# A matmul with a decayed running sum: from the fifth pair of chunks on, x is turned by transposing DMAs, and the output leaves in lumps of eight slots

## The chip, the cores and the metric

The kernel runs on one core of a Trainium2 chip. The metric is the time of one execution on the device in microseconds (us). The engines are named as in the profile: PE (TensorE, the matmuls), PEld (its weight loads), DVE (VectorE), ACT (ScalarE), POOL (GpSimd) and SP (SyncE, which here only issues DMAs). SP, ACT and POOL each have a queue of their own from which they start DMAs; an engine works through its instructions in order.

## What is computed

```python
B, S, D = (16, 2048, 1024)          # x: (16, 2048, 1024), w: (1024, 1024), decay: (1024,)
xw = x @ w
out[:, 0, :] = xw[:, 0, :]
for t in range(1, S):
    out[:, t, :] = decay[None, :] * out[:, t - 1, :] + xw[:, t, :]
```

All inputs and the output are float32. The kernel multiplies in bfloat16 and sums in float32.

## The kernel before

The work is cut into 64 chunks of 512 time steps (`TL`), four for each of the 16 batches. Two chunks make a group; there are 32 groups. For each group the kernel goes through eight column blocks `n` of 128 output columns each. One (group, block) pair is a slot; the last group is done chunk by chunk, so there are 31 x 8 + 2 x 8 = 264 slots. PE computes in one slot the product for 128 output columns (on the partitions) and 1,024 time steps: 8 pieces of the inner dimension times 2 chunks, 16 matmuls of 512 columns.

**How x gets in.** The matmul needs x with its inner dimension on the partitions. `load` (L105) brings one quarter of a chunk with one DMA from POOL, casting float32 to bfloat16: 32 partitions hold time steps, and a run is 256 columns of x, so four DMAs make a chunk in a tile `xb` (ring of 3). `turn` (L115) is a DVE transpose in blocks of 32 x 32 of pairs of bfloat16 into `xw` (ring of 2). `part` (L123) is an ACT copy in two halves that separates the pairs into `xt` (ring of 5), which the matmuls (L131) read. The partition order that comes of this is matched by the order in which w lies in `wsb`.

**What happens to a product.** Two kinds of slot alternate by a fixed rule. In an unpaired slot DVE runs the scan with the decay straight from PSUM (L221). In a paired slot, of which there are three in four, ACT copies the product to `xs` (L183) and makes decay times the even steps (L169); POOL adds them to the odd steps (`join`, L196); DVE scans only the odd steps with the square of the decay (L201); ACT multiplies again (L169), and POOL fills in the even steps (`fill`, L246). The last value of each row is kept for the next group of the same batch (L250). Then `back` (L258) turns the result on DVE in 32 x 32 blocks into an output tile `ot`.

**How the output gets out.** An `Outlet` collects four slots in one `ot` tile (ring of 4). When its fourth slot has been turned, `store` (L282) issues four DMAs of 512 KB from SP, one for each quarter of the partitions, with runs of 512 bytes in DRAM. Only at the end of the run some stores go out from POOL as well.

**What sets the order.** Every operation is pinned in program order on its engine. After each slot's matmuls, `perform` runs a list of deeds, each a letter with a number: P (copy, even part, join), S (scan), C (complete), B (back), T (turn a chunk), X and Y (its two part copies), L (one load). For slots 0 to 33 and for the last 20 the lists are written out by hand (`agenda`); between them `usual` makes them, and `later` says at which slot T, X and Y of a chunk come: 11, 10 and 8 slots ahead of the group's first slot for its first chunk, 7, 6 and 4 for its second. After T of chunk c the loads of chunk c+3 are put in line, and L takes them one or two a slot. At the end `ending` turns the last tiles on PE and stores them in four DMAs with rows of 2 KB (L393).

Of the kernel before, what the change touches and what calls it, by code (L numbers as in the profile page):

```python
# [22 lines left out]


@with_exitstack
def kernel(
# [7 lines left out]

# [38 lines left out]
    dec = const.tile([128, K], FP32, name="dec")  # L89
    squares = [const.tile([128, K], FP32, name="squares")]  # L90
    wsb = const.tile([128, K, K, NQ, P], BF16, name="wsb")
    wcols = wsb.rearrange("p k (h r) q i -> p k h q r i", h=2)

    def ot_tile(nj):
        return ring(sb, "ot", 4, [128, nj, CR])
# [4 lines left out]

    def load(c, q, j0=0, j1=NJ):
        b, t0 = chunks[c]
        if c not in xb_of:
            xb_of[c] = ring(sb, "xb", 3, [128, NJ, CQ], BF16)
        pin(nc.gpsimd.dma_start(  # L105
            out=xb_of[c][quad(q), j0:j1],
            in_=_ap(x, [[D, P], [P * D, j1 - j0], [1, CQ]],
                    (b * S + t0 + j0 * P) * D + q * CQ)))

# [9 lines left out]
    def part(c, copy, m0, m1, j0=0, j1=NJ):  # L119
        if c not in xt_of:  # L120
            xt_of[c] = ring(sb, "xt", 5, [128, M, 2, TL], BF16)
        src = xw_of[c][:, m0:m1, j0:j1].rearrange("p m j i e -> p m e (j i)")
        pin(copy(out=xt_of[c][:, m0:m1, :, j0 * P:j1 * P], in_=src))  # L123

    def matmul(ps, n, k, xt, t0=0, t1=TL, start=0, pairs=None):
# [4 lines left out]
        lhs = wsb[:, k, n].rearrange("p q i -> p (q i)")  # L130
# [10 lines left out]
    class Tile:  # L141

        def __init__(self, g, n, ps, outlets):
            self.b, self.t0 = chunks[g[0]]
            self.T = TL * len(g)
            self.n, self.ps, self.outlets = n, ps, outlets
            self.paired = n % R != R - 1
# [17 lines left out]
        def decayed(self, src):  # L167
# [3 lines left out]
                scale=dec[:, self.n:self.n + 1]))  # L171
# [26 lines left out]
        def scan(self):  # L198
            T, n, so = self.T, self.n, self.so
            if self.paired:  # L200
                pin(nc.vector.tensor_tensor_scan(  # L201
                    out=so[:, 3:T + 2:2],
                    data0=squares[-1][:, n:n + 1].to_broadcast([128, T // 2]),
# [11 lines left out]
        def run(self, ps, t, size):  # L215
            n, so = self.n, self.so
            if t:
                before = so[:, t + 1:t + 2]
            else:
# [3 lines left out]
                data0=dec[:, n:n + 1].to_broadcast([128, size]),  # L223
# [28 lines left out]
        def back(self, half=None):  # L252
            n, c0 = self.n, self.n % R * P
            for outlet in self.outlets:
                if half not in (None, outlet.half):
                    continue
                t0, nj = outlet.t0, outlet.nj
                pin(nc.vector.transpose(  # L258
# [7 lines left out]
    class Outlet:  # L266


        def __init__(self, ns, nj, half=0, queues=(nc.sync,), pieces=1):
            self.pieces = pieces  # L270
            self.ns, self.missing, self.half = ns, set(ns), half
            self.nj, self.t0, self.queues = nj, half * nj * P, queues
            self.ot = ot_tile(nj)

        def store(self, b, t0):
            n0 = self.ns[0]
            c0 = n0 % R * P
            size = len(self.ns) * P
            nj = self.nj // self.pieces
            for j in range(0, self.nj, nj):  # L280
                for i, q in enumerate((0, 2, 1, 3)):
                    pin(self.queues[i % len(self.queues)].dma_start(  # L282
                        out=_ap(out, [[D, P], [P * D, nj], [1, size]],
                                (b * S + t0 + self.t0 + j * P) * D
                                + n0 // R * CH + q * CR + c0),
                        in_=self.ot[quad(q), j:j + nj, c0:c0 + size]))


# [63 lines left out]
    def decays(i):  # L352
        pin(nc.vector.transpose(out=cols, in_=rows))
        pin(nc.vector.tensor_copy(
            out=dec.rearrange("p (h r) -> p h r", h=2), in_=cols[:, :, 0:R]))
        square(0)

    def square(i):
        pin(nc.vector.tensor_tensor(
            out=squares[-1][:, 0:K], in0=dec, in1=dec, op=ALU.mult))  # L360
# [4 lines left out]


# [8 lines left out]
    def ending(i):  # L375
# [7 lines left out]
        def cross(blocks, rs):  # L383
# [6 lines left out]
        def leave(i, copy):  # L390
# [3 lines left out]
                out=_ap(out, [[D, 128], [1, CH]], (b * S + t0 + i * 128) * D + CH),  # L394
                in_=wides[i].rearrange("p q r i -> p (q r i)")))

        cross((0,), range(R))
        cross((1,), range(R))
        cross((2, 3), range(R - 1))
        cross((2, 3), (R - 1,))  # L400
# [7 lines left out]
    def turn_and_load(c):  # L408
        turn(c)
        if 2 <= c < nch - 3:  # L410
            loads.extend((c + 3, q) for q in range(NQ))
# [9 lines left out]
        "Y": lambda c: part(c, nc.scalar.copy, 2, M),  # L421
        "x": lambda c: part(c, nc.vector.tensor_copy, 0, 2),
# [35 lines left out]
        9: "k6 h6 c5 B4",  # L458
# [9 lines left out]
        19: "S16 j17 p18 B15 L g18 L S17 k16 h16 z18 j18",  # L468
        20: "Y7 S19 L c16 k17 h17 T8 k19 L c17",
        21: "p20 g20 L S18 X8 j20 B17 B19",  # L470
        22: "L h18 p21 c18 B16 k18 g21 B18 Y8 z20 L j21 S20",
        23: "p22 z21 z22 S21 L h20 g22 T9 c20 h21",
        24: "k21 k20 j22 S23 X9 L c21 Y9 B20 L",
        25: "B23 k23 p24 B21 g24 z24 j24 S22 z25",
        26: "p25 T10 k22 h22 g25 c22 S24 X10 j25",
        27: "B22 p26 S25 g26 z26 Y10 j26",
        28: "S27 h25 h24 c25 S26 c24",
        29: "B27 h26 c26 T11 p28 g28 j28 B24",
        30: "p29 B25 g29 z28 j29 S28 z29 S29",
        31: "h28 p30 c28 B26 g30 h29 B28 j30 z30",  # L480
        32: "c29 S31 S30 h30 B29 c30 p32 g32 z32 j32 B30 B31 L L",
        33: "p33 g33 z33 j33 S32 h32 c32 k32 L L",
# [23 lines left out]
    begun = {"T": 12, "X": 11, "Y": 11}  # L506
    for c in range(5, nch):
        first = c // 2 * K
        ahead = (7, 6, 4) if c % 2 else (11, 10, 8)
        for letter, a in zip("TXY", ahead):  # L510
            if c >= begun[letter]:
                later.setdefault(first - a, []).append(f"{letter}{c}")

    def usual(s):
# [11 lines left out]
        return do + later.get(s, []) + ["L"] * (2 if len(loads) > NQ else 1)  # L526

    def rest(s):
# [4 lines left out]
        return do + [f"B{s - 1}"] + later.get(s, []) + ["L"] * len(loads)  # L533
# [7 lines left out]
    for step, (g, n) in enumerate(slots):  # L541
        T = TL * len(g)
        left = step - len(slots)
        if n % R == 0:
# [95 lines left out]
```

## Time and profile before

| | |
|---|---|
| two timed runs | 908.58 and 909.44 us, median 909.01 |
| profiled execution, first to last instruction (its span) | 907.2 us |
| profiled execution, what lies around the span | not listed; the median of the runs is 1.8 us above the span |
| granted TensorE clock, mean | 0.998 |
| busy: PE / DVE / ACT / POOL | 892.8 / 826.3 / 686.2 / 663.0 us |
| matmuls L131 of 512 columns from `xt` | 859.8 us, 3,914 records |
| ACT copies L123 of 2,048 elements | 124, 1,904 ns each |
| DVE turns L115 of a whole chunk | 62, 2,285 ns each |
| DVE turns L258 of 1,024 steps | 248, 1,216 ns each |
| POOL issuing a load L105 | 264, 661 ns each |
| POOL issuing an output L282 | 8, 722 ns each |
| loads, 256 KB written each, issue to landing | 248, 7.8 us in the median |
| outputs, 512 KB each, issue to landing | 244 from SP, 10.9 us in the median |

All times come from one profiled execution on one core. "Busy" is the time in which an engine had an instruction running; a DMA that an engine issues is not counted in it. The page cuts the span into 40 slices of 22.7 us and gives the busy share of each in tenths. Landing is the time from a DMA's issue until its data have arrived. In the lists of waits the name left of the arrow is the engine that waited and the name right of it is what came last.

### The profile page before, as it was taken

What the parts mean: (1) busy time and instruction counts of PE and PEld (TensorE: products, weight loads), DVE (VectorE), ACT (ScalarE), POOL (GpSimd) and SP (SyncE); (2) the same over time, 40 slices, a digit from 0 to 9 for tenths busy, and PEclk for the clock granted to TensorE, in tenths of its full rate; (3) what the DMA queues carried; (4) which work ended last, traced back from release to release, by engine and by line L of the source; (5) the groups of instructions that cost most, each with busy time, mean ns of one, the idle gap of its engine ahead of it and who ended that gap; (6) DMA issues with size and microseconds to landing.
All of it is one profiled execution on the core that took longest, in us unless ns stands there. A gap on an engine that the chain in (4) does not pass through costs nothing.

```text
span 907.2 us, 12004 instructions
## 1 busy us (share of the span) xinstructions
PE 892.8 (98%) x4119; PEld 411.4 (45%) x4201; DVE 826.3 (91%) x628; ACT 686.2 (76%) x955; POOL 663.0 (73%) x763
## 2 busy tenths in 40 slices
PE   9999999999999999999999999999999999999996
PEld 5444444444444444444444444444444444444443
DVE  4999989999999999899999999999999999999996
ACT  4889867777777877877877778778778778777742
POOL 7888678877777767768677777777677686776562
PEclk9999999999999999999999999999999999999999
DMA  9999999999999999999999999999999999999788
GB/s 194 194 215 220 227 215 220 215 238 255 249 250 254 241 243 259 247 244 228 227 233 227 227 232 227 226 232 233 220 230 231 228 231 223 232 229 207 153 161 211
DMA packets 397230, 204.77 MB, mean 226 GB/s; under 512 B 8816, under 2 KB 395376, under 8 KB 397168
## 3 DMA queue, kind: packets, MB, share of 16 engines
q1 hardware_dynamic: 258960, 131.62, 59.6%
q0 software_dynamic: 137920, 71.85, 58.1%
q8 instruction: 33, 0.54, 0.2%
q10 hardware_dynamic: 288, 0.52, 0.2%
q14 instruction: 29, 0.24, 0.1%
HBM read 138.42 MB, written 134.22 MB: 301 GB/s over the span
## 4 chain that ended last, share of the span: by engine, by line
PE 93%; DMA 2%; POOL 1%; issue 1%; DVE 1%; ACT 0%; POOLq 0%; DVEq 0%
PE ps L131 93%; DMA xb<-in_x_dram 2%; POOL ot L299 1%; POOL xb L105 1%; PE spare L131 1%; DVE xw L115 0%; ACT xt L123 0%; ACT xs L183 0%; DVE so L201 0%; PE spare L387 0%; DVE ot L258 0%; ACT h L169 0%; PE ps L387 0%; POOLq L635 0%; POOL xs L196 0%
## 5 line engine op out<-in xcount | busy, mean ns | idle before, releaser
L131 PE MATMUL ps<-xt,wsb 128*128 128x512 bf16 x3942 | 863.5, 378 | 4.7 <-ACT h L169 0.2
L131 PEld LDWEIGHTS <-wsb 128*128 128x128 bf16 x4152 | 405.9, 98 | 479.9 <-ACT wsb L306 0.8
L196 POOL TENSOR_TENSOR xs<-h,xs 128x512 f32<-128x512 f32 (+1 forms) x190 | 243.0, 1279 | 181.8 <-ACT h L169 79.4
L183 ACT COPY xs<-ps 128x1024 f32<-128x1024 f32 (+1 forms) x190 | 189.4, 997 | 155.3 <-PE ps L131 144.2
L258 DVE STREAM_TRANSPOSE ot<-so 128x1024 f32<-128x1024 f32 (+1 forms) x260 | 300.1, 1191 | 2.1 <-POOL so L190 1.1
L246 POOL TENSOR_TENSOR so<-h,xs 128x512 f32<-128x512 f32 (+1 forms) x190 | 241.4, 1272 | 39.0 <-ACT h L169 25.7
L123 ACT COPY xt<-xw 128x2048 bf16<-128x2048 bf16 (+1 forms) x136 | 242.3, 1790 | 7.8 <-DVE xw L115 7.6
L105 POOL DMA_DIRECT2D xb<-in_x_dram x264 | 174.3, 661 | 3.3 <-DMA ot<-in_w_dram 1.1
L169 ACT ACTIVATE h<-so,dec 128x512 f32<-128x512 f32 (+1 forms) x190 | 145.4, 766 | 27.7 <-DVE so L201 24.4
L115 DVE STREAM_TRANSPOSE xw<-xb 128x2048 f32<-128x2048 f32 (+1 forms) x78 | 147.4, 1901 | 5.5 <-DMA xb<-in_x_dram 5.5
L201 DVE TENSOR_TENSOR_SCAN so<-spare,keep,xs 128x512 f32<-128x512 f32 (+1 forms) x97 | 120.0, 1239 | 27.7 <-POOL xs L196 27.4
L201 DVE TENSOR_TENSOR_SCAN so<-spare,xs 128x512 f32<-128x512 f32 x93 | 113.3, 1220 | 27.6 <-POOL xs L196 24.6
L169 ACT ACTIVATE h<-ps,dec 128x512 f32<-128x512 f32 (+1 forms) x190 | 130.3, 686 | 0.0
L221 DVE TENSOR_TENSOR_SCAN so<-dec,ps 128x1024 f32<-128x1024 f32 x34 | 76.8, 2261 | 1.0 <-ACT h L169 1.0
L221 DVE TENSOR_TENSOR_SCAN so<-dec,keep,ps 128x1024 f32<-128x1024 f32 (+1 forms) x35 | 75.9, 2169 | 0.1
L250 ACT COPY keep<-so 128x1 f32<-128x1 f32 x136 | 25.3, 189 | 9.9 <-DVE so L221 9.4
L192 ACT COPY so<-keep 128x1 f32<-128x1 f32 x97 | 18.4, 191 | 2.6 <-DVE ot L258 2.4
L131 PE MATMUL ps<-xw,wsb 128*128 128x256 bf16 (+1 forms) x68 | 11.2, 301 | 0.1
L190 POOL MEMSET so<- 128x1 f32 x93 | 10.7, 117 | 0.6 <-DVE ot L258 0.6
L131 PE MATMUL spare<-xt,wsb 128*128 128x512 bf16 (+1 forms) x48 | 10.0, 335 | 0.0
L282 POOL DMA_DIRECT2D out_dram<-ot x8 | 5.7, 722 | 5.5 <-DVE ot L258 5.1
L299 POOL DMA_DIRECT2D ot<-in_w_dram x12 | 6.6, 546 | 3.3 <-DMA xb<-in_x_dram 2.0
(38 smaller groups left out, 44.5 us busy)
## 6 DMA issues: line engine op xcount, KB each, us to landing
out_dram<-ot SPq DMA_DIRECT2D x244, 512.0 KB, 10.9
xb<-in_x_dram POOLq DMA_DIRECT2D x248, 256.0 KB, 7.8
xb<-in_x_dram POOLq DMA_DIRECT2D x16, 128.0 KB, 5.8
out_dram<-ot POOLq DMA_DIRECT2D x4, 512.0 KB, 11.6
ot<-in_w_dram POOLq DMA_DIRECT2D x12, 128.0 KB, 5.1
out_dram<-ot SPq DMA_DIRECT2D x4, 256.0 KB
out_dram<-ot POOLq DMA_DIRECT2D x4, 256.0 KB, 8.5
out_dram<-ot SPq DMA_DIRECT2D x8, 128.0 KB, 4.3
```

The source lines that it names most:

```text
L105: pin(nc.gpsimd.dma_start(out=xb_of[c][quad(q), j0:j1], in_=_ap(x, [[D, P], [P * D, j1 - j0], [1, CQ]], (b * S + t0 + j0 * P) * D + q * CQ)))
L115: pin(nc.vector.transpose(out=dst.rearrange("p (m j i) -> p j m i", m=M, i=P)[:, j0:j1, m0:m1], in_=src.rearrange("p (j m c) -> p j m c", ...
L123: pin(copy(out=xt_of[c][:, m0:m1, :, j0 * P:j1 * P], in_=src))
L131: pin(nc.tensor.matmul(out=ps[:, t0:t1] if ps.shape[1] >= t1 else ps, lhsT=lhs, rhs=rhs, start=(k == 0 and t0 == start), stop=(k == K - 1),))
L169: pin(nc.scalar.activation(out=h, in_=src, func=mybir.ActivationFunctionType.Copy, scale=dec[:, self.n:self.n + 1]))
L183: pin(nc.scalar.copy(out=self.xs, in_=self.ps))
L196: pin(nc.gpsimd.tensor_tensor(out=odds, in0=self.g, in1=odds, op=ALU.add))
L201: pin(nc.vector.tensor_tensor_scan(out=so[:, 3:T + 2:2], data0=squares[-1][:, n:n + 1].to_broadcast([128, T // 2]), data1=self.xs[:, 1:T:2 ...
L221: pin(nc.vector.tensor_tensor_scan(out=so[:, t + 2:t + 2 + size], data0=dec[:, n:n + 1].to_broadcast([128, size]), data1=ps, initial=befor ...
L246: pin(nc.gpsimd.tensor_tensor(out=self.so[:, 2:T + 2:2], in0=self.h, in1=self.xs[:, 0:T:2], op=ALU.add))
L250: pin(nc.scalar.copy(out=self.keep, in_=self.so[:, self.T + 1:self.T + 2]))
L258: pin(nc.vector.transpose(out=outlet.ot[:, :, c0:c0 + P], in_=self.so[:, 2 + t0:2 + t0 + nj * P].rearrange("p (i t) -> p i t", t=P)))
```

## The change

From chunk 8 (group 4, slot 32) on:

- A chunk of x is loaded by one DMA from POOL in whole rows of 4 KB, 128 time steps on the partitions, four such row blocks in the `xb` tile. SP then issues four transposing DMAs (`cross`), each of which takes one block of 128 rows x 1,024 bfloat16 from `xb` to `xt`, with 8 x 128 elements on each of 128 partitions. `turn` and `part` are no longer used for these chunks.
- The four transposes of a chunk come 7 slots (first chunk of a group) or 5 slots (second chunk) ahead of the group's first slot. The load of chunk c+3 is placed three slots behind the transposes of chunk c, whose `xb` buffer it takes.
- The inner dimension now lies in plain order and so do the output columns, so a second copy of the weights, `wsn`, is made in slots 19 to 31: two loads (N) and eight ACT copies (n). The decay and its square get a second copy as well (A).
- For groups 4 to 29 an outlet is a lump of eight slots: 1,024 columns and 1,024 time steps, 4 MB, in 1-KB runs. The `ot` ring is two lumps. When the lump is full, SP issues the quarters 0 and 2 at once; the quarters 1 and 3 are put in line, and POOL issues one of them in each of the next slots (O).
- `xt` has a ring of 4 in place of 5.
- The last tiles, turned on PE, go to DRAM in four runs of 512 bytes a row in place of one of 2 KB.

```diff
+    FIRST = 8
+    WIDE = range(FIRST // 2, nch // 2 - 2)
+
+    def crossed(c):
+        return c >= FIRST
+
+    def column(c, n):
+        return n * P if crossed(c) else n // R * CH + n % R * P
+
+    SPAN = {False: CR, True: CQ}
...
+    wsn = const.tile([128, K, K, NQ, P], BF16, name="wsn")
...
-    def ot_tile(nj):
-        return ring(sb, "ot", 4, [128, nj, CR])
+    def lump():
+        return ring(sb, "ot", 2, [128, 2, 2 * NJ * CR])
...
     def load(c, q, j0=0, j1=NJ):
         b, t0 = chunks[c]
         if c not in xb_of:
             xb_of[c] = ring(sb, "xb", 3, [128, NJ, CQ], BF16)
+        if crossed(c):
+            pin(nc.gpsimd.dma_start(
+                out=xb_of[c].rearrange("p (l j) c -> p l (j c)", l=NB),
+                in_=_ap(x, [[D, 128], [128 * D, NB], [1, D]], (b * S + t0) * D)))
+            return
...
+    def cross(c):
+        xt_of[c] = ring(sb, "xt", 4, [128, M, 2, TL], BF16)
+        rows = xb_of[c].rearrange("p (l j) c -> p l (j c)", l=NB)
+        cols = xt_of[c].rearrange("p m e t -> p (m e) t")
+        for l in range(NB):
+            pin(nc.sync.dma_start_transpose(
+                out=cols[:, :, l * 128:(l + 1) * 128], in_=rows[:, l]))
...
         def store(self, b, t0):
+            if len(self.ns) == K:
+                for q in (0, 2):
+                    self.send(nc.sync, q, b, t0)
+                for q in (1, 3):
+                    due.append(lambda q=q: self.send(nc.gpsimd, q, b, t0))
+                return
...
+        def send(self, queue, q, b, t0, j=0, nj=None):
+            nj = nj or self.nj
+            pin(queue.dma_start(
+                out=_ap(out, [[D, P], [P * D, nj], [1, len(self.ns) * P]],
+                        (b * S + t0 + self.t0 + j * P) * D
+                        + q * SPAN[crossed(self.c)] + column(self.c, self.ns[0])),
+                in_=self.ot[quad(q), j:j + nj]))
...
+    def fetch(i):
+        part = ring(sb, "xw", 2, [128, NB, D], BF16)
+        for l in range(NB):
+            wst[i * NB + l] = part[:, l]
+        pin(nc.gpsimd.dma_start(
+            out=part, in_=_ap(w, [[D, 128], [128 * D, NB], [1, D]], i * NB * 128 * D)))
+
+    def place(k):
+        pin(nc.scalar.copy(
+            out=wsn[:, k].rearrange("p n q i -> p q n i"),
+            in_=wst[k].rearrange("p (q n i) -> p q n i", q=NQ, n=K)))
...
             pin(nc.sync.dma_start(
-                out=_ap(out, [[D, 128], [1, CH]], (b * S + t0 + i * 128) * D + CH),
-                in_=wides[i].rearrange("p q r i -> p (q r i)")))
+                out=_ap(out, [[D, 128], [CQ, NQ], [1, CR]], (b * S + t0 + i * 128) * D + CR),
+                in_=wides[i].rearrange("p q r i -> p q (r i)")))
...
     def turn_and_load(c):
-        turn(c)
+        if crossed(c):
+            cross(c)
+        else:
+            turn(c)
         if 2 <= c < nch - 3:
-            loads.extend((c + 3, q) for q in range(NQ))
+            loads.extend((c + 3, q) for q in range(1 if crossed(c + 3) else NQ))
...
-    begun = {"T": 12, "X": 11, "Y": 11}
-    for c in range(5, nch):
-        first = c // 2 * K
-        ahead = (7, 6, 4) if c % 2 else (11, 10, 8)
-        for letter, a in zip("TXY", ahead):
-            if c >= begun[letter]:
-                later.setdefault(first - a, []).append(f"{letter}{c}")
+    for c in range(FIRST, nch):
+        at = c // 2 * K - (5 if c % 2 else 7)
+        later.setdefault(at, []).append(f"T{c}")
+        later.setdefault(at + 3, []).append("L")
...
-        return do + later.get(s, []) + ["L"] * (2 if len(loads) > NQ else 1)
+        return do + later.get(s, []) + ["O"] * (len(due) > 0)
...
-        if n % R == 0:
-            ns, nj = range(n, n + R), T // P
+        lot = K if g[0] // 2 in WIDE else R
+        if n % lot == 0:
+            ns, nj = range(n, n + lot), T // P
...
             for k, l in todo:
-                matmul(ps[:, l * TL:(l + 1) * TL], n, k, xt_of[g[l]])
+                matmul(ps[:, l * TL:(l + 1) * TL], n, k, xt_of[g[l]],
+                       of=wsn if crossed(g[l]) else wsb)
```

## The prediction

> **What bounds the kernel now.** I read the page's busy shares first, then the slices, the chain that ended last, the queue table, and last the waits of SP's own queue.
>
> ```profile
> PE 892.8 (98%) x4119; PEld 411.4 (45%) x4201; DVE 826.3 (91%) x628; ACT 686.2 (76%) x955; POOL 663.0 (73%) x763
> ...
> PE   9999999999999999999999999999999999999996
> ...
> DMA  9999999999999999999999999999999999999788
> GB/s 194 194 215 220 227 215 220 215 238 255 249 250 254 241 243 259 247 244 228 227 233 227 227 232 227 226 232 233 220 230 231 228 231 223 232 229 207 153 161 211
> ...
> q1 hardware_dynamic: 258960, 131.62, 59.6%
> q0 software_dynamic: 137920, 71.85, 58.1%
> ...
> PE 93%; DMA 2%; POOL 1%; issue 1%; DVE 1%; ACT 0%; POOLq 0%; DVEq 0%
> ```
>
> TensorE is busy in every slice but the last, and the chain is 93% TensorE. A busy PE need not be at its peak, so I checked the rate in the chain in order of time:
>
> ```profile
> 59.10 10.96 PE ps L131 x50
> 70.11 10.74 PE ps L131 x49
> ```
>
> The second piece is 49 matmuls in 10.74 us and the next starts 10.79 us after it: about 216 ns for each 512-column matmul, without a hole. A group of two chunks is 128 matmuls, 27.6 us, and a slot 3.45 us. So DVE, ACT and POOL work beside PE, and their work is worth nothing in time until it makes PE wait. The other thing to see is that the DMA engines too are busy in nine tenths of every slice; the shares of the two queues add up to 118%, so their packets overlap.
>
> The third view is what SP does, because the change puts new work there:
>
> ```profile
> SPq L282 <- DVE ot L258: 299.9, 50, 33.6
> ```
>
> ```profile
> L282 SPq DMA_DIRECT2D out_dram<-ot x256: 315/2622/6642, 38.7 to 900.2; - x128
> ...
> DMA to landing us min/median/max: 3.5/10.8/19.0
> ```
>
> The first line: SP spends 300 of 907 us waiting for DVE's output turns. The second (ns, min/median/max): one output DMA holds SP for 0.3 to 6.6 us, 2.6 in the median, and lands 10.8 us after issue. SP is a queue in order; whatever stands behind an output there waits with it.
>
> **The change, part by part** (durations from the groups by form, one group = 27.6 us).
>
> DVE loses 56 turns L115 of 2,285 ns (128 us); ACT loses 112 copies L123 of 1,904 ns (213 us) and gains 8 copies for the second set of weights, about 1 us each by half that row. POOL issues 1 load a chunk in place of 4 at 0.661 us: 56 x 3 x 0.66 = 111 us less, and 26 groups x 2 outputs x 0.72 us = 37 us more. All of this lies beside PE: worth 0. Matmul count and weight loads (98 ns each, under 216) stay: 0. The first 8 chunks keep their order: 0. Once only come four decay DMAs of 1 KB on SP (slot 9) and two loads of the second weights on POOL (slots 19 and 21, 0.66 us each; the second waits for the last turned chunk's copy in slot 20): hidden by the same POOL idle time, 0. At the very end four stores go from 2-KB rows to 512-byte runs, 512 runs each; at the mean time of a 512-byte packet below that is 512 x 33.4 / 16 = 1.1 us each, where 2.7 to 3.3 us is their time to land now: 0 to +2 us, I take +1.
>
> DMA engines. From the queue table: an output packet of 512 bytes takes 0.596 x 16 x 907.2 us / 258,960 = 33.4 ns, a load packet 61 ns. Outputs become half as many packets of 1 KB. The packet records of the trace have 98 ns for the few 2,048-byte packets of the same queue, so by a line through both a 1-KB one costs about 55 ns: 4,096 of them a group, 225 against 274 us of engine time. Loads read 4-KB rows: a quarter of the packets; between 61 ns (as now) and 4 x 61 ns each, 62 to 250 us a group against 250. New are 2 MB a group turned from SBUF to SBUF: 8 DMAs, each with 1,024 runs of 256 bytes at its destination.
>
> The price of one such DMA is what the trace does not show. Low end: the shortest output issue, 0.32 us, if nothing but SP's issue counts. High end: the longest, 6.6 us. Between them, by run count: 1,024 runs is also what one output DMA has. At the same price a run, 1,024 x 33.4 / 16 = 2.14 us; shortened along the line through the 512- and 2,048-byte packets, 22.6 ns a run, 1.45 us. I take t = 1.8 us, midway, because neither row reorders data and the run count is what is alike.
>
> The Trainium skill has two rules here that speak against each other. "DMA: Bandwidth & Descriptors", section "Latency and other measured facts", gives 261 GB/s for a transposing DMA; estimated from it, 256 KB takes 1.0 us and the sum below would be no loss. "VectorE: DVE Perf Modes", section "The three transpose paths", gives 1,309 ns for one 128x128 block; estimated from it, 8 blocks one after another take 10.5 us and the transposes alone 84 us a group. No run so far shows either.
>
> The path this sits on. The output of group m-1 (a lump) is complete when DVE has turned its last tile. In the trace that tile's scan starts at 303.46 us, about 1 us after its matmuls, and the last output turn ends at 309.10: 6.7 us after PE left the lot. Then SP issues two quarters of the lump (2 x 2.6 = 5.2), and only behind them, in program order, the 8 transposes of group m+1 (slots 1 and 3), whose data also lie behind the 2 MB of output in the same queue. They must have landed when PE ends group m. So from PE's end of group m-1: 6.7 + 5.2 + 8t + 3.5 (shortest landing) = 15.4 + 8t, against 27.6. Break-even is t = 1.52 us. At 1.8: 29.8, PE waits 2.2 us a group (at 0.32 no wait, at 6.6 41 us). This holds for groups 6 to 31, 26 x 2.2 = 57 us. Groups 4 and 5 are worse: the store before their transposes is still four DMAs on SP (10.5 us): 6.7 + 10.5 + 14.4 + 3.5 = 35.1, 7.5 us each, 15 us. Two other waits I cost at nothing. The load three slots behind waits on POOL until its buffer's transposes have read it (even chunk: done at 6.7 + 5.2 + 7.2 + 3.5 = 22.6 us, POOL there at about 19): up to 4 us, twice a group. Joins and fills, and so DVE's scans, queue behind it. Its cover is POOL's idle time, 27.6 - 20.6 busy + 2.5 freed = 9.5 us a group, and three ps tiles; if that cover is gone it is up to 8 us a group. The lump ring of two: POOL's last quarter is issued near 6.7 + 2 slots = 13.6 us and is needed back at 34.5; with 11.6 us landing for half its size today, at most 23.2, it could be 2 us late; DVE has the 4.6 us a group freed to absorb it.
>
> Sum: 907.2 (span) + 57 + 15 + 1 = 980; the median of the runs is 1.8 us over the span, so 982 us.
>
> **Rivals.**
> Hidden (not slower): t stays under 1.52 us, or SP's outputs issue in the 0.3 us minimum instead of the median. For it: SP's 300 us of waiting, and the bytes to be moved rise only from 6.3 to 8.4 MB a group, 304 GB/s where single slices show 259. Against: three costs in series in front of one deadline, with no slack left at the median rows. Time: 907.2 + 1.8 + 1 = 910, and at t = 1.52 twice 5.3 us more at groups 4 and 5: 910 to 921.
> By a sentence of the Trainium skill this is the expected case: "Advanced Engine Details and Errata", section "X-Bar Transpose (TRN2)", calls transposing DMAs as fast as regular ones. The trace, having no such DMA, cannot agree or differ.
>
> Dear transposes: t at the high end, 6.6 us: 15.4 + 53 = 68 us a group, +41 x 26, and 2 x 46 at groups 4 and 5: 2,060 us; at t = 3, 11.8 x 26 + 2 x 17 more: 1,251. For it: turning moves each 2-byte element to another partition, which no row of the trace prices. Against: only that the longest output issue was a queue that was full. The Trainium skill's rule of 1,309 ns ("VectorE: DVE Perf Modes", as above) leads here and past it, by its estimate.
>
> DMA engines as the bound: if the load packets cost 4 x 61 ns, the group needs 225 + 250 + 8,192 x 22.6 to 33.4 ns (185 to 274) = 660 to 749 us of engine time against 524 today in 27.6 us; if 524 is already the most that fits, 34.8 to 39.4 us a group, +7.2 to +11.8 x 26: 1,097 to 1,217. Against: nothing shows that 524 is the limit, since SP and the loads keep up.
>
> Faster: the most there is to gain is what PE does not do: 907.2 - 892.8 = 14 us, nearly all in the start and the tail, which stay. Over 2% would be under 891.
>
> **Numbers.** Late transposes by the queue order (t from 1.6 to 2.3): 50%, 937 to 1,094 us. Hidden: 27%, 906 to 921 (its low end gives back a third of the 14 us in which PE does not work). DMA engines bound: 10%, 1,097 to 1,217. Dear: 12%, above 1,094, mostly above 1,200. Faster by over 2%: 1%. Predicted 982. The range 906 to 1,190 leaves out most of the dear case and a little of the bound one; the forecast's own range is 937 to 1,094. A difference of 2% is about what a measurement of this kernel can tell from no change: faster 1%, within 2% 27%, slower 72%.
>
> **What would show it.** Right: in the chain, PE pieces broken at the start of every group by a wait for xt from a transposing DMA, 2 us each, 7 at groups 4 and 5; ACT and DVE idle far more (ACT under 55%, DVE under 80%); SP's transposes right behind two outputs. Wrong: pieces of 10.74 us unbroken to the end and the wait of SP for DVE still long (hidden); SP busy throughout, transposes back to back of 3 us or more (dear); loads or outputs landing much later than 7.8 and 10.8 us while SP is free (engines). The forecast falls first with t, then with the 5.2 us of outputs ahead of it.

## The result, and the profile after

The changed kernel takes 1,367.55 us (two runs, 1,363.15 and 1,371.94); before it was 909.01. The ratio is 1.504, with a 95% interval of 1.493 to 1.516. The profiled execution took 1,363.15 us, its span is 1,361.2 us. The direction was forecast, the size was not: 982 us with a range up to 1,190.

The page of the changed kernel, the lines that answer to those shown of before:

```profile
PE 959.0 (70%) x4119; PEld 422.5 (31%) x4201; DVE 707.9 (52%) x575; ACT 494.8 (36%) x851; POOL 601.9 (44%) x649
...
PE   9996675686657845785668567856587566866697
...
PEclk9998787897879877987788778877897779877899
DMA  9999999999999999999999999999999999999998
GB/s 194 211 227 240 233 187 175 218 202 182 197 175 209 191 174 171 201 195 177 178 206 180 174 175 200 200 176 197 195 203 201 178 177 209 193 195 186 188 199 234
...
q1 hardware_dynamic: 334864, 135.83, 53.3%
q0 software_dynamic: 64416, 128.46, 49.0%
...
PE 41%; SPq 29%; DMA 23%; issue 3%; DVE 2%; POOL 1%; ACT 1%; POOLq 0%; DVEq 0%; ACTq 0%
```

From the fourth slice on PE has holes in all slices but one, and its granted clock falls to 0.7 to 0.9. ACT, DVE and POOL have become far idler, as forecast, and it is worth nothing. The DMA row says 9 in all but the last slice, much as before. The two queue shares add up to 102%, where the kernel before had 118%: packets are under way nearly all the time, and yet fewer of them side by side.

Who waited, in all (waiter, its line, what came last, us in total, times, longest):

```profile
PE ps L151 <- DMA xt<-xb: 362.0, 46, 19.1
POOL xb L113 <- DMA xt<-xb: 347.8, 40, 15.1
```

L151 are the matmuls, L127 the transposes, L113 the whole-row loads, L311 the stores. PE waits 362 us for transposed x, 13 us for each of the 28 groups that use it: the place that the forecast named, with five times the size. POOL waits almost as long in its loads.

The transposes themselves (ns, min/median/max of what one holds SP; then us to landing):

```profile
L127 SPq DMA_TRANSPOSE xt<-xb x224: 1232/3504/9737, 117.7 to 1326.9; - x112
...
DMA to landing us min/median/max: 2.7/9.5/18.3
```

One group in order of time (start, us, what; in brackets the idle time before it and what ended it):

```profile
810.66 30.37 PE L151 MATMUL ps<-xt,wsn 128*128 128x512 bf16 x125 [11.84 <-DMA xt<-xb]
...
811.11 0.79 POOL L113 DMA_DIRECT2D xb<-in_x_dram  x1 [6.33 <-DMA xt<-xb]
...
811.91 1.29 POOL L267 TENSOR_TENSOR so<-h,xs 128x512 f32<-128x512 f32 x1
...
813.24 2.37 DVE L280 STREAM_TRANSPOSE ot<-so 128x1024 f32<-128x1024 f32 x2 [5.14 <-POOL so L267]
...
815.64 0.92 SPq L311 DMA_DIRECT2D out_dram<-ot  x2
...
816.67 31.27 SPq L127 DMA_TRANSPOSE xt<-xb  x8
...
856.58 2.74 PE L151 MATMUL ps<-xt,wsn 128*128 128x512 bf16 x6 [10.45 <-DMA xt<-xb]
```

Read from the top: the group's transposes have landed, so PE starts, and POOL's load, which waited for the same transposes, is let go. Only then comes the last fill L267, behind the load on POOL; DVE turns it; the lump is full and SP stores; behind the stores come the eight transposes of the next group, 31 us of issuing, and 9 us later PE can start again. It looks like a closed chain of 46 us, with everything hanging on everything.

### The profile page after: what moved, and what is told of

It reads as the page before. It is cut to its first block, busy times and chain, and to the rows that moved or that the text cites. A ratio compares the mean times of both kernels' runs of the same rounds, so it can differ in the third digit from the quotient of the medians.

```text
span 1361.2 us, 11850 instructions
## 1 busy us (share of the span) xinstructions
PE 959.0 (70%) x4119; PEld 422.5 (31%) x4201; DVE 707.9 (52%) x575; ACT 494.8 (36%) x851; POOL 601.9 (44%) x649
## 4 chain that ended last, share of the span: by engine, by line
PE 41%; SPq 29%; DMA 23%; issue 3%; DVE 2%; POOL 1%; ACT 1%; POOLq 0%; DVEq 0%; ACTq 0%
PE ps L151 40%; SPq L127 27%; DMA xt<-xb 19%; DMA out_dram<-ot 3%; SPq L311 2%; DVE ot L280 1%; DVE so L242 1%; DVE so L222 1%; DMA xb<-in_x_dram 0%; DMA ot<-in_w_dram 0%; POOL xb L117 0%; SPq L398 0%; POOL xs L217 0%; ACT h L190 0%; POOL out_dram L311 0%
## 5 line engine op out<-in xcount | busy, mean ns | idle before, releaser
L151 PE MATMUL ps<-xt,wsn 128*128 128x512 bf16 x3488 | 831.5, 399 | 391.0 <-DMA xt<-xb 362.0
L151 PEld LDWEIGHTS <-wsn 128*128 128x128 bf16 x3592 | 363.1, 102 | 865.0 <-issue 417.1
L280 DVE STREAM_TRANSPOSE ot<-so 128x1024 f32<-128x1024 f32 (+1 forms) x260 | 303.6, 1197 | 141.2 <-POOL so L267 82.1
L267 POOL TENSOR_TENSOR so<-h,xs 128x512 f32<-128x512 f32 (+1 forms) x190 | 240.5, 1267 | 36.7 <-ACT h L190 25.4
L113 POOL DMA_DIRECT2D xb<-in_x_dram x56 | 43.9, 784 | 452.4 <-DMA xt<-xb 347.8
L151 PE MATMUL ps<-xt,wsb 128*128 128x512 bf16 (+1 forms) x454 | 99.3, 374 | 1.1 <-DVE wsb L334 0.5
L151 PEld LDWEIGHTS <-wsb 128*128 128x128 bf16 x560 | 54.4, 97 | 58.5 <-issue 1.4
L311 POOL DMA_DIRECT2D out_dram<-ot x60 | 47.6, 794 | 5.1 <-DVE ot L280 5.1
L143 ACT COPY xt<-xw 128x512 bf16<-128x512 bf16 (+1 forms) x24 | 29.1, 1256 | 5.9 <-DVE xw L135 5.9
L117 POOL DMA_DIRECT2D xb<-in_x_dram x40 | 25.2, 634 | 3.4 <-DMA ot<-in_w_dram 0.9
L135 DVE STREAM_TRANSPOSE xw<-xb 128x256 f32<-128x256 f32 (+1 forms) x22 | 19.4, 923 | 5.6 <-DMA xb<-in_x_dram 5.6
L151 PE MATMUL ps<-xw,wsb 128*128 128x256 bf16 (+1 forms) x68 | 11.2, 301 | 0.6 <-DVE xw L135 0.6
## 6 DMA issues: line engine op xcount, KB each, us to landing
out_dram<-ot SPq DMA_DIRECT2D x52, 1024.0 KB, 10.3
out_dram<-ot POOLq DMA_DIRECT2D x52, 1024.0 KB, 11.7
```

Source lines behind the costliest of these rows:

```text
L113: pin(nc.gpsimd.dma_start(out=xb_of[c].rearrange("p (l j) c -> p l (j c)", l=NB), in_=_ap(x, [[D, 128], [128 * D, NB], [1, D]], (b * S + t ...
L151: pin(nc.tensor.matmul(out=ps[:, t0:t1] if ps.shape[1] >= t1 else ps, lhsT=lhs, rhs=rhs, start=(k == 0 and t0 == start), stop=(k == K - 1),))
L267: pin(nc.gpsimd.tensor_tensor(out=self.so[:, 2:T + 2:2], in0=self.h, in1=self.xs[:, 0:T:2], op=ALU.add))
L280: pin(nc.vector.transpose(out=outlet.ot[:, :, c0:c0 + P], in_=self.so[:, 2 + t0:2 + t0 + nj * P].rearrange("p (i t) -> p i t", t=P)))
L311: pin(queue.dma_start(out=_ap(out, [[D, P], [P * D, nj], [1, len(self.ns) * P]], (b * S + t0 + self.t0 + j * P) * D + q * SPAN[crossed(sel ...
```

## The experiments

Theory A took that chain at its word: the loops of waits cost the time. Theory B: the DMA engines cannot pass this traffic faster, and the waits only show where one stands while it passes. Theories C (transposes slow by themselves), D and E (slow beside other packets) are named as they come in. Each time below is of one execution, with the kernel before at 908.2 to 908.8 us on the same chip; the changed kernel is compared at 1,363 us, its profiled execution. "Sum" is that of the two queue shares; times the span it is the time that all packets took, on 16 engines. That time holds what packets wait for one another, so it is no fixed price of the traffic: e9 moves as many packets and bytes as the changed kernel, in 1,533 us of it in place of 1,393.

| run | us | sum of shares | packet time, us |
|---|---|---|---|
| kernel before | 909 | 117.7% | 1,068 |
| changed kernel | 1,363 | 102.3% | 1,393 |
| e1 loads six slots behind | 1,252 | 103.7% | 1,297 |
| e2 no lump stores | 945 | 89.4% | 843 |
| e3 lumps all from POOL | 1,295 | 109.4% | 1,415 |
| e4 first transposes ahead of the stores | 1,250 | 108.2% | 1,350 |
| e5 as e4, all stores on SP | 1,344 | 105.1% | 1,410 |
| e6 as e5, loads in four pieces | 1,385 | 114.0% | 1,577 |
| e7 as e5, loads six behind | 1,283 | 107.4% | 1,376 |
| e8 all stores at once on SP | 1,347 | 100.6% | 1,353 |
| e9 transposes read one chunk | 1,395 | 110.1% | 1,533 |
| e10 as e9, order of e4 | 1,362 | 108.4% | 1,475 |
| e11 half the lump stored | 1,123 | 100.1% | 1,122 |
| e12 half the transposes | 1,195 | 103.9% | 1,240 |
| e13 copies for transposes | 1,206 | 102.5% | 1,235 |
| e14 transposes bundled | 1,220 | 106.7% | 1,300 |
| e15 before + spare transposes | 1,340 | 120.8% | 1,616 |
| e16 before + spare copies | 1,244 | 116.4% | 1,446 |
| e17 e1 and e4 together | 1,394 | 111.5% | 1,552 |
| e18 before + few spare copies | 962 | 118.7% | 1,140 |

**Order and traffic, first look.** The load six slots behind the transposes:

```diff
-        later.setdefault(at + 3, []).append("L")
+        later.setdefault(at + 6, []).append("L")
```

> The load of chunk c+3 stands six slots behind the transposes of chunk c, not three. Theory A (a loop through POOL closes every group: POOL waits in a load until the transposes have landed, the last fill stands behind that load, the lump's stores wait for the fill, and the next transposes stand behind the stores on SP): POOL's 448 us of waiting before L113 mostly go, the loop then spans two groups, (48 + 28) / 2 = about 39 us a group in place of 44: 1,230 to 1,280 us. Theory B (the DMA engines are full, 102% of shares): no change, 1,350 to 1,375. Theory C (the transposes are slow by themselves, 25 us for four): no change or as A, since only their place is moved.

1,252 us: within the range that A gave, and against B.

```diff
                 if len(self.ns) == K:
-                for q in (0, 2):
-                    self.send(nc.sync, q, b, t0)
-                for q in (1, 3):
-                    due.append(lambda q=q: self.send(nc.gpsimd, q, b, t0))
                     return
```

> The stores of the 26 lumps (groups 4 to 29) are left out, so that part of the output is not written; all else stays. A: nothing stands ahead of the transposes on SP and POOL's wait is short: 905 to 930 us, transposes of 1.3 us each back to back, landing under 5 us. B: also far lower, 905 to 1,000, since half the traffic is gone. C: four transposes still take 20 us and more, 1,200 or above.

945 us, in B's range and 15 above A's. This settles C, because here the transposes can be seen with no store beside them (one stretch of 100 us; ns on SP and us to landing):

```profile
L127 SPq DMA_TRANSPOSE xt<-xb x31: 1232/1307/4693, 603.5 to 699.9; - x31
...
DMA to landing us min/median/max: 2.8/3.1/3.7
```

So 256 KB hold SP for 1.3 us, less than the 1.8 us that the forecast took. Transposes are not slow by themselves.

```diff
-                for q in (0, 2):
-                    self.send(nc.sync, q, b, t0)
-                for q in (1, 3):
+                for q in range(NQ):
                     due.append(lambda q=q: self.send(nc.gpsimd, q, b, t0))
```

> All four quarters of a lump go out from POOL, one a slot; the same traffic, but SP holds only transposes. A: the transposes no longer wait for the stores, 910 to 970 us. B: same traffic, same time, 1,340 to 1,380. C: at least 1,200.

```diff
-                for q in (0, 2):
-                    self.send(nc.sync, q, b, t0)
-                for q in (1, 3):
-                    due.append(lambda q=q: self.send(nc.gpsimd, q, b, t0))
+                for queue, q in ((nc.sync, 0), (nc.sync, 2), (nc.gpsimd, 1), (nc.gpsimd, 3)):
+                    due.append(lambda q=q, queue=queue: self.send(queue, q, b, t0))
```

> The two quarters from SP are put in line like the others, so the first chunk's transposes stand ahead of them on SP and the second chunk's behind. A: the first four transposes run early, the second four behind 2 MB of stores and beside POOL's: the next group's start is 25 to 32 us after the group before the last ended, 930 to 1,020 us. B: same traffic, 1,340 to 1,380. C: at least 1,200.

1,295 and 1,250 us. Neither A nor B gave these (C's "at least 1,200" covers them, but e2 speaks against C): some 70 and 110 us come back, not the 340 and more of A. With SP free of stores (e3) the transposes still held SP for up to 17.9 us each.

**Who slows the transposes?** Two stretches of the changed kernel from the DMA view (packets, MB, share of 16 engines): 829 to 834 us, transposes (q1) beside POOL's packets (q0), then 844 to 847 us, transposes alone.

```profile
q0 software_dynamic: 228, 0.88, 79.3%
q1 hardware_dynamic: 404, 0.10, 24.4%
```

```profile
q1 hardware_dynamic: 3102, 0.77, 119.9%
```

Beside POOL's packets they move 20 KB a us, alone 257, in most of its slices 280 and more. So theory D: POOL's large packets starve them.

```diff
-                for q in (0, 2):
-                    self.send(nc.sync, q, b, t0)
-                for q in (1, 3):
-                    due.append(lambda q=q: self.send(nc.gpsimd, q, b, t0))
+                for q in (0, 2, 1, 3):
+                    due.append(lambda q=q: self.send(nc.sync, q, b, t0))
```

> As the run with the first chunk's transposes ahead of the stores (1,250 us), with one difference: the two quarters that POOL stores are stored by SP, at the same places in the order. Theory D (turn-taking: beside a packet of POOL's queue, 2 or 4 KB and 160 to 170 ns, each DMA engine passes one 256-byte packet of a transpose, so the transposes move 22 KB/us where alone they move 280; POOL's stores starve them): with the 4-KB packets gone only the loads, 11 us a group, starve the transposes: 920 to 1,030 us. Theory B (engines full, all traffic alike): the same traffic, 1,230 to 1,270. A third way, order alone: more stores stand on SP, so 1,250 to 1,330.

e6 was this with each load cut into four pieces of 256 columns, e7 with `at + 6` as in e1.

> All stores on SP as before it, and each chunk's load cut into four pieces of 256 columns, so that the loads' packets are 512 bytes of about 60 ns, four times as many (15 us of engine time a group in place of 11). D: beside them the transposes pass 256 bytes in 78 ns, about 50 KB/us, so they suffer less: 10 to 60 us less than with whole rows if starving by the loads still costs anything, at most 20 more if not. B: more packets, 20 to 60 us more.

> All stores on SP, and loads six slots behind the transposes. D together with the loop through POOL (A): POOL does not wait any more and nothing starves the transposes but the loads, 910 to 960 us. B: 1,230 to 1,270.

```diff
-                for q in (0, 2):
-                    self.send(nc.sync, q, b, t0)
-                for q in (1, 3):
-                    due.append(lambda q=q: self.send(nc.gpsimd, q, b, t0))
+                for q in (0, 2, 1, 3):
+                    self.send(nc.sync, q, b, t0)
```

> The changed kernel with one part undone, the two queues: all four quarters leave from SP when the lump is full, ahead of all transposes. D with A: the loop stays (fill behind the load, stores behind the fill, transposes behind 4 MB of stores), but the transposes run at their own pace once the stores are out: 5 + 2 + 12 + 9 + 3 and up to 5 for a load, 31 to 36 us a group in place of 44, 1,000 to 1,150 us. B: 1,340 to 1,390. Order alone: more stands ahead of the transposes, 1,400 or above.

1,344, 1,385, 1,283 and 1,347 us. D falls as the cause of the time: with no store on POOL e5 is 94 us slower than e4, e7 is 31 us slower than e1, and e8 is 16 us faster than the changed kernel. B has e8 in its range and e6 (41 us over e5, where it gave 20 to 60), misses e7 by 13 us and e5 by 74: the same traffic in another order did not take the same time. What D said of the rate is right all the same. Two stretches of e8 from the DMA view, the first with transposes alone, the second where a load has come in:

```profile
q1 hardware_dynamic: 3729, 0.92, 102.8%
```

```profile
q0 software_dynamic: 422, 0.86, 91.7%
q1 hardware_dynamic: 339, 0.09, 10.9%
```

In 821 to 825 us the transposes move 0.92 MB in 4 us. In 826 to 832 they move 0.09 MB in 6 us: 339 packets beside 422 load packets, of 256 bytes against 2 KB, each queue about one in turn. The Trainium skill has this rule ("DMA: Bandwidth & Descriptors", "Queues, rings and completion order": an engine takes turns between queues by packets); the trace agrees. The load passes 0.86 MB in that time, at 208 ns a packet, not far from the median of 173 in that run: the load loses little, the transposes nearly all.

**Are the waits the cause at all?** In e9 all transposes read the buffer of chunk 8 and the loads go to two other buffers, so that no load waits for a transpose and no transpose for a load; e10 adds the order of e4.

```diff
-        if c not in xb_of:
+        if c > FIRST:
+            xb_of[c] = sb.tile([128, NJ, CQ], BF16, name=f"xb{(c + 1) % 2}")
+        elif c not in xb_of:
...
-        rows = xb_of[c].rearrange("p (l j) c -> p l (j c)", l=NB)
+        rows = xb_of[FIRST].rearrange("p (l j) c -> p l (j c)", l=NB)
```

> All transposes from chunk 9 on read the buffer of chunk 8, and the loads go to two other buffers that nothing reads (later chunks' x is left out of the result); all traffic and every place in the order stay. No load waits for a transpose any more, no transpose for a load. A (loops of waits): POOL never waits, what is left is the order on SP, as with loads six slots behind or better, 1,100 to 1,250 us. B (the DMA engines' time: a group needs 4,096 store packets, 8,192 transpose packets and 1,024 load packets, 702 us of engine time by their mean times in the changed kernel, 44 us on 16 engines): 1,250 to 1,370.

> The same (later chunks' x left out), and the first chunk's transposes ahead of the stores on SP. A: no loop left that spans less than two groups, 910 to 1,010 us. B: 1,100 to 1,260, at the lower end if the mean times of the packets fall with less waiting side by side (46 ns a store packet, 18 a transpose packet, 172 a load packet, each at its median, are 511 us of engine time, 32 us a group, 1,030 us: nothing below that).

1,395 and 1,362 us. A falls in the form that was tested: POOL's 348 us of waiting for transposes are gone, the traffic is the same, and the kernel is no faster. The waits of stores for the last turn, of transposes on SP behind stores and of PE for transposes are still there, and PE's have grown (waits of e9):

```profile
PE ps L153 <- DMA xt<-xb: 424.1, 29, 27.6
```

B has neither run in its range: e9 is 25 us above it, e10 102 us. The gain of e1 was then no proof of A; e17, e1 and e4 together, later took 1,394 us. The two gains do not add up, as they would if each had removed a wait of its own.

Then less traffic, with the waits left as they are: e11 stores two of four quarters (the `for q in (1, 3)` loop is taken out), e12 transposes two of a chunk's four row blocks and lets ACT copy the others.

> Quarters 1 and 3 of each lump are not stored (half the output of groups 4 to 29 is left out). B: 120 us of engine time less a group, 7.6 us x 26, 1,150 to 1,180 us. A with turn-taking beside POOL's stores: POOL's stores were what held the first four transposes for 10 us and more, 1,050 to 1,130.

> Two of the four row blocks of each chunk are transposed, the other two only copied by ACT (half of x is not turned). B: 4,096 transpose packets less, 4,096 x 30 / 16 = 7.8 us a group, 1,140 to 1,180. A: the loop loses two transposes of the first chunk (12 us of 25) and two of the second (2.6 us), 960 to 1,080.

1,123 and 1,195 us: 240 and 168 us less than 1,363. B is off by some 30 and 15 us, to one side and to the other. For e11 the answer of A with turn-taking, 1,050 to 1,130, is the one that holds; for e12 A's is 115 us too low, though there SP also waited 159 us for ACT, which has the added copies, so that e12 changes a wait as well. Traffic moves the time, but a packet is not worth the same everywhere.

**Transposes, or any traffic?** The deciding runs. e13 is the changed kernel with plain copies of the same bytes and runs; e15 is the kernel before with four spare transposes a chunk that nobody reads, e16 the same with spare copies, and e18 with one spare copy a chunk. The edits of e13, of e15 and of e16 (e18 has 1 for its 4):

```diff
-            pin(nc.sync.dma_start_transpose(
-                out=cols[:, :, l * 128:(l + 1) * 128], in_=rows[:, l]))
+            pin(nc.sync.dma_start(
+                out=cols[:, :, l * 128:(l + 1) * 128],
+                in_=rows[:, l].rearrange("p (k t) -> p k t", t=128)))
```

```diff
     def turn_and_load(c):
         turn(c)
+        for l in range(4 if c >= 8 else 0):
+            pin(nc.sync.dma_start_transpose(
+                out=aside[l],
+                in_=wsb[:, l].rearrange("p n q i -> p (n q i)")))
```

```diff
     def turn_and_load(c):
         turn(c)
+        for l in range(4 if c >= 8 else 0):
+            pin(nc.sync.dma_start(
+                out=aside[l],
+                in_=wsb[:, :, l].rearrange("p k q i -> p k (q i)")))
```

> The changed kernel with each transposing DMA replaced by a plain copy of the same 256 KB in the same 1,024 runs of 256 bytes, same places and waits (so x is not turned). E (transposes pass at 280 KB/us only with the engines to themselves, at 20 to 35 KB/us beside any other packets, and hold those up): a copy does not have that, 920 to 1,030 us. B (engine time by packets, whatever they do): 1,300 to 1,370. A (loops of waits): in between, as the copies land sooner, 1,000 to 1,200.

> The kernel before, and beside its own work 224 transposing DMAs of 256 KB from SP, four at each turn of a chunk from chunk 8 on, out of the weights into a buffer that nothing reads: no new wait but the places on SP's queue. E: stores and loads now run beside transposes and are held up, 1,150 us or more. B: 524 + 8,192 x 18 to 30 ns of engine time a group, 35 to 40 us at the overlap of before, 1,110 to 1,250. A: 910 to 930, since no loop is closed.

> The same with plain copies of the same size in runs of 256 bytes in place of the transposes. E: 910 to 1,000 us, far from the run with spare transposes. B: the same as that run. A: 910 to 930.

> The kernel before with one spare copy of 256 KB a chunk in place of four. B, if the kernel before stands right at the engines' limit: a quarter of the 336 us that four cost, 84 us, 980 to 1,000 us. If it has room that four copies overran: less than 20 us, 910 to 930.

1,206 us for e13; 1,340 for e15; 1,244 for e16; 962 for e18. No theory comes through whole. A is out by 300 us and more in e15 and e16 and by 6 in e13. E has e15 but not e13, and not e16, which it put at 1,000 us at most. B is 94 us too high in e13 and 90 too low in e15, e16 was to equal e15, and e18 lies between its two answers. What is left of B is that traffic which nobody reads costs time. The queue lines of e16, then of e15:

```profile
q1 hardware_dynamic: 491920, 190.35, 72.2%
q0 software_dynamic: 137920, 71.85, 44.2%
```

```profile
q1 hardware_dynamic: 495504, 190.37, 77.4%
q0 software_dynamic: 137920, 71.85, 43.4%
```

The sums are 116% and 121%, beside 118% before: traffic came on top, and the run grew longer in place of the sum. That packet time grows 1.35 times and the run 1.37 times is the same statement, not a second proof; the packet records give one: the spare copies took 22.5 ns each in the mean, 322 us on 16 engines, and the run grew by 336. So the kernel before stood nearly at what the engines pass of such a mix. No instruction waits for these copies. What PE waits for there is the rest of the work behind the engines (waits of e16):

```profile
DVE ot L259 <- DMA out_dram<-ot: 400.8, 55, 17.1
...
PE ps L132 <- DVE so L222: 228.8, 52, 12.5
```

DVE waits for an output tile that is still being stored, and PE for a product that DVE has not scanned.

A rival is SP's queue: the copies (L412) stand on it in order with the outputs (L283). These are SP's lines in e16 (ns, min/median/max), its wait for DVE, which was 299.9 us before, and then the HBM lines of the pages, before and e16:

```profile
L412 SPq DMA_DIRECT2D aside<-wsb x224: 677/2720/7592, 108.1 to 1210.5; - x112
L283 SPq DMA_DIRECT2D out_dram<-ot x256: 337/2190/6005, 38.9 to 1236.0; - x128
...
SPq L283 <- DVE ot L259: 53.1, 15, 33.8
...
HBM read 138.42 MB, written 134.22 MB: 301 GB/s over the span
...
HBM read 138.42 MB, written 134.22 MB: 219 GB/s over the span
```

SP is held almost all the time. But at their shortest these issues would hold it some 240 us in all, so what holds it lies behind it. By the packet records, from about 140 us on and without the last 100 us, at least 16 packets were in flight on the 16 engines for 87% of the time in e16 (93% before) and fewer than 8 for 2% (under 0.1% before): the engines had work. In e2, where PE ran almost without a break, they had fewer than 8 for 24%. Nor is it HBM: the copies go from SBUF to SBUF, and the HBM rate fell.

One copy a chunk (e18) costs 54 us where a quarter of four would be 84: a room of some 30 us, 3%, was all there was. In the kernel before, then, 336 of the 431 us that spare transposes cost are traffic as such, and that it transposes adds 95 (e15 against e16); in the changed kernel transposing adds 157 (1,363 against 1,206). The packet records put this on the 256-byte packets: 18 ns each in the median both times, but 30.3 in the mean in the changed kernel and 19.2 in e13, a difference of 160 us on 16 engines.

**Keeping them apart.** e14 puts all eight transposes of a group together, the loads three slots behind, and the stores, all on SP, from the third slot of a group on.

```diff
-                for q in (0, 2):
-                    self.send(nc.sync, q, b, t0)
-                for q in (1, 3):
-                    due.append(lambda q=q: self.send(nc.gpsimd, q, b, t0))
+                for q in (0, 2, 1, 3):
+                    due.append(lambda q=q: self.send(nc.sync, q, b, t0))
...
-        at = c // 2 * K - (5 if c % 2 else 7)
+        at = c // 2 * K - 8
...
-        return do + later.get(s, []) + ["O"] * (len(due) > 0)
+        return do + later.get(s, []) + ["O"] * (len(due) if s % K >= 2 else 0)
```

> All eight transposes of a group stand together at the start of the group before, all four store quarters behind them on SP, and both loads three slots after, so that as little as can be runs beside the transposes. E: 8 us of transposes, then stores and loads side by side, 364 us of engine time or 22 us at the overlap of the kernel before, 30 to 33 us a group, 970 to 1,080 us. B: same packets, 1,230 to 1,370.

> The changed kernel with both re-orderings that helped alone: the first chunk's transposes ahead of the stores, the loads six slots behind. B in two parts (the packets' time is 1,390 us, and the two queues pass 1.18 us of it in a us only while both have work side by side; 1.02 in the changed kernel): with less waiting on one another the sum of the shares rises to 108 to 115%, 1,190 to 1,250 us. A (the waits are what costs): both gains add up, 1,130 to 1,150 or less.

1,220 us for e14, the best order with all the traffic in place, though still 311 us over the kernel before, and a new wait shows: DVE for output tiles still being stored, 135 us. B misses it by 10 us, E by 140 (E's 22 us is 364 over 16 engines with no overlap; with that of before it is 19). At 1,394 us, e17 is 144 us above B's range and further above A's. So the order alone moves the time between 1,220 and 1,394 us with all the traffic in place, and I found no rule that says which way. Empty engines do not explain it: fewer than 8 packets were in flight for 1% of the time in e17 and for 4% in e14 (8% in the changed kernel), while a transpose packet took 38.6 ns in the mean in e17 and 25.3 in e14.

## Why the prediction was wrong

- *PE bound, and idle ACT, DVE and POOL worth nothing*: right. ACT fell to 36%, DVE to 52%, both under the marks that were set.
- *The place*: right. PE breaks at the start of every group and waits for xt.
- *The DMA engines* is the step that failed: the sum put the engines' time at nothing, because "nothing shows that 524 is the limit, since SP and the loads keep up". e16 and e18 show that the engines were nearly full: 58.7 MB of copies that nothing reads cost the kernel before 336 us, and a quarter of them 54, so that the room was some 30 us. The 118% of before was read as "their packets overlap" and not as engines that are nearly full. In this kernel, loads that keep up and a DMA row of nines were how that looked; that SP waited 300 us for DVE spoke of SP and not of the engines. The terms of the rival were near the mean packet times of the changed kernel: stores 225 us of engine time a group (243), loads 62 to 250 (210), transposes 185 to 274 (249), together 660 to 749 (702). These means include waiting; at the medians the same packets are 511 us.
- *The rival's time* was wrong too. It was held at 10%, with 1,097 to 1,217 us, and the measured time is above it, where the dear case stood. e13 lands in it with 1,206, but by luck: its sum of shares is 102.5% and not 118%, and its packets took 1,235 us and not 1,393.
- *The signs that were set* did not tell the rivals apart: transposes of 3.5 us in the median read as the dear case, and loads of four times the size and outputs of twice the size land in 9.3 and in 10.3 to 11.7 us, hardly later than the 7.8 and 10.8 that were named. It took e2, where a transpose holds SP for 1.3 us, and e16 to tell the dear case from the engines.
- *What that rival lacked* is the sum of shares falling from 118% to 102%. 1,393 us of packet time at 117.7% would be 1,183 us; the other 178 us come with fewer packets side by side. That 702 us over 16 engines is 43.9 us, and the groups follow each other at about 44, only says the same as a sum near 100%. The measured part of the cause is that traffic costs, and transposing more than copying; why the queues pass less together stays open: e9 and e10 had more side by side (110 and 108%), but each transpose packet took longer (35.0 and 33.6 ns in the mean against 30.3), and the time did not fall.
- *t = 1.8 us* was too high undisturbed (1.3) and too low beside stores and loads (3.5 in the median, 9.7 at most; landing 9.5 us in place of the 3.5 that the sum used). In the group shown, the path from the first transpose to PE's start took 39.9 us, where the sum had 8t + 3.5 = 17.9. A price that depends on what passes beside it was taken as one number.
- *The loop* was written with an error: the path of group m+2 starts at the end of group m, so behind a wait ahead of group m+1 there is none ahead of m+2. The path spans two periods, and a delay of 2.2 us would have cost 1.1 a group, about 28 us in place of 57. It does not matter against 454.
- *The load three slots behind at nothing*: wrong in the chain (POOL waited 348 us, and the cover of 9.5 us a group was gone), but taking this wait away did not help by itself: e9 is no faster, though e1, which moves the loads, is by 111 us.
- *Not in the sum at all*: PE's clock. The main matmuls took 399 ns in place of 379 and PE was busy 66 us longer, at a granted clock of 0.849 in place of 0.998. No run separates what this cost; if the engines set the pace, what PE is busy longer it waits less.
- *The rules weighed*: that of the Trainium skill, "as fast as regular" ("Advanced Engine Details and Errata", "X-Bar Transpose (TRN2)") did not hold beside other traffic, by the 95 and 157 us above. The 261 GB/s of the Trainium skill ("DMA: Bandwidth & Descriptors", "Latency and other measured facts") is near what they reach alone, 0.92 MB in 4 us, 230 GB/s. The Trainium skill's 1,309 ns for one 128x128 block ("VectorE: DVE Perf Modes", "The three transpose paths") would make eight blocks one after another 10.5 us, as an estimate. A DMA of eight such blocks landed in 3.1 us in the median in e2; it held SP for 1,307 ns, and that this is so near may be chance.

## What to carry to other kernels

Before moving work from engines to DMAs, add up the queue shares, and where the DMA row shows nines suspect that the engines are full, even if no queue waits; a few spare copies that nobody reads measure the room in one run. Do not read the cause off a chain of waits: cut the waits with the traffic left in place, and cut the traffic with the waits left in place. And a kernel whose bound engine has no holes has nothing to gain from freeing the others, only something to lose.

## What the runs showed of the hardware

- A transposing DMA of 256 KB holds SP 1.3 us and lands in about 3 us with little beside it; with a load beside it, 0.09 MB passed in 6 us.
- Spare plain copies in 256-byte runs from SBUF to SBUF, 58.7 MB in all, cost the kernel before 336 us; their packets took 322 us on 16 engines. Over the whole run the sum of queue shares stayed at 116 to 121% in e15, e16 and e18. It is no fixed ceiling: in the kernel before, 30 to 40 us, it was 157% at 191 GB/s, and 123% at 251 GB/s from 200 to 300 us.
- A 256-byte transpose packet took 18 ns in the median in all these runs, but 20.3 ns in the mean without the stores (e2), 30.3 in the changed kernel and 38.6 in e17; as a plain copy it took 19.2 (e13).
- PE's mean granted clock was 0.849 in the changed kernel, where PE waited 13 us a group for x, against 0.998 before.
